# Projections of 512 tokens a matmul beside a top-256 search, with a pooling map folded into its weights

## The chip, the core and the metric

The kernel runs on one core of a Trainium2 chip. The metric is the device time of one execution in microseconds. Three runs of the kernel before took 4264.55, 4264.18 and 4262.73 us; the median is 4264.18 us.

## What is computed

One layer of an encoder over 4096 tokens of 1024 channels. Cut to what matters:

```python
h = rms_norm(x, norm_g)
q, k, v, qi, ki, wi, z_a, u_b, z_b, gates = split(h @ w_in)
# search: for each token the 256 best keys
iscore = einsum('bqhs,bqh->bqs', relu(einsum('bqhd,bsd->bqhs', qi, ki)), wi)
_, idx = top_k(where(allowed, iscore, -inf), 256)
a = softmax_attention(q, k[idx], v[idx]) * silu(z_a)
# pooling: per group g of 128 channels, window w in (2, 4, 8, 16)
pooled = (cumsum(u_b) - lagged) / count - u_b
b = (einsum('bsgc,gcd->bsgd', pooled, pool_w) * pool_scale) * silu(z_b)
y = sigmoid(g_a) * (a @ w_branch_a) + sigmoid(g_b) * (b @ w_branch_b)
out = x + y @ w_out
```

The sums over tokens and the map pool_w act on different axes, so the map may stand before or behind the sums.

## The kernel before

There are four stages. The first (up to 442.9 us of the span) norms x, projects q, k, v and the search's queries and keys, and writes h to DRAM as a high and a low part (hD). The second holds two independent pieces of work side by side: the search, and the remaining projections with their epilogues. The third is the attention, the fourth the branch products and the output. Only the second is touched, and the loads for it at the end of the first.

Products of full float32 precision are made of three: high by high, high by low and low by high.

**The projections** (`dense`). There are 28 units, each 128 columns of w_in: u and zb for four pooling groups, 16 gates a and b, and four za. They are done in sweeps over all tokens: in the first four sweeps u, zb and three gates, in the last two four gates or za. A sweep goes through the tokens in chunks of 256: two tiles h (high, low) of 1 MB are loaded for a chunk, twice buffered, and every unit of the sweep makes 24 matmuls on them, 8 k by 3 products of 128x256, into a PSUM tile pd (lines 1052 to 1054). The weights of a sweep are loaded (wraw) and split into wgh (ACT) and wgl (POOL). Those of the first sweep are loaded at the end of the first stage (`on_early`).

**Epilogues.** A gate is a sigmoid on ACT and a store (gD). The pooling (`pool`) copies u (ACT), adds shifted copies of it (POOL), subtracts the token (DVE), splits the result into ph and pl (ACT, POOL), multiplies by pool_w on PE (three matmuls of 256 columns, lines 347 to 349, with the split map wm), and multiplies by scale and silu (DVE, line 983).

**The search.** For each query block of 128 tokens, keys in pieces of 1024: PE makes the scores of a head (line 765, tile ps), ACT takes the relu (rl), DVE multiplies by the head's weight and adds into ring (line 770). POOL fills ring beforehand (iota, line 753). Blocks are collected into groups; seven rounds on ACT (line 855) and DVE find each row's threshold, and `finish` takes the last candidates (lines 883 and 884) and writes the bias, 0 or -1e30, in bf16 (line 902, on DVE), stored in pieces (biasD). A block's first threshold comes from `guess`, which needs the last block's keys, by a reload of what the first stage stored (r31, k31); its matmul is line 635.

**The order.** Every step is handed to a planner (`Plan`) with an engine, a cost, a key and the steps before it. The planner plays the program through with those costs: on each engine it starts the ready step with the smallest key whose tiles have a free buffer. What comes out is a fixed order on each engine, SP's queue of DMAs included. On the chip each engine works its order through strictly, and waits where a step is not ready. The costs and keys thus decide only the order. At the end of the stage the matmul of line 1074 counts rows whose threshold was not unique, a branch reads it, and the attention starts behind the branch.

## Time and profile before

| | |
|---|---|
| median of three runs | 4264.18 us |
| the profiled execution | 4264.02 us |
| its span | 4262.3 us |
| PE, DVE, ACT, POOL busy over the span | 97%, 75%, 55%, 45% |
| granted TensorE clock, mean | 0.987 of full speed |

The times of single instructions come from this one execution, counted from the span's start. A busy time of PE contains the drain of each matmul, which lies beside the next one: a matmul of 256 columns is shown with 0.28 us though the next starts 0.12 us after it. Distances between starts tell what PE can do. In a name such as pd<-h,wgh the tile written stands first; buffer numbers are left out. A wait is shown behind `<-` with the engine, tile and line that ended it.

### The profile page before, as it was taken

The page shows a single profiled execution, that of the slowest core. Times are in us where ns is not written, and L with a number is a line of the kernel's source. Part 1 is how long each engine was busy: PE and PEld are TensorE (multiplying, and loading weights), DVE is VectorE, ACT ScalarE, POOL GpSimd, SP SyncE. Part 2 cuts the span into 40 slices and gives each one's busy share as a digit, 9 for nine tenths or more (in the row PEclk, how much of TensorE's full clock was granted, in tenths as well). Part 3 has the DMA queues.
Part 4 walks back from the last instruction along what each step waited for, and adds up shares of the span by engine and source line. Part 5 has one row for each costly group of instructions (what it writes and reads, how often), then busy time and mean ns, then how long its engine had stood idle before and what let it go on. Part 6 is the DMA issues. An engine that isn't in the chain of part 4 may idle for free.

```text
span 4262.3 us, 76690 instructions
## 1 busy us (share of the span) xinstructions
PE 4137.7 (97%) x27746; PEld 3492.4 (82%) x27747; DVE 3217.1 (75%) x7786; ACT 2344.9 (55%) x3977; POOL 1903.4 (45%) x1717
## 2 busy tenths in 40 slices
PE   8999899999999999999799999999999999999999
PEld 7988799899999998999756666666666658999998
DVE  5554688889899888788679999999999995434342
ACT  5444588767877877887455555555555552111110
POOL 3455222323234333010047888888999991111110
PEclk9999999999999999999899999999999999999999
DMA  6666644545444446565543212212111016544442
GB/s 227 242 239 233 208 156 169 176 172 184 166 174 164 163 168 196 204 233 200 190 85 72 57 45 49 48 47 52 42 41 39 23 42 190 163 134 151 137 144 77
DMA packets 442041, 586.32 MB, mean 138 GB/s; under 512 B 148861, under 2 KB 337849, under 8 KB 437434
## 3 DMA queue, kind: packets, MB, share of 16 engines
q1 hardware_dynamic: 441658, 581.39, 42.0%
q8 instruction: 219, 3.59, 0.3%
q14 instruction: 164, 1.34, 0.1%
HBM read 388.54 MB, written 175.54 MB: 132 GB/s over the span
## 4 chain that ended last, share of the span: by engine, by line
PE 47%; DVE 1%; DMA 1%; POOL 1%; issue 0%; ACT 0%; SPq 0%; DVEq 0%; POOLq 0%; ACTq 0%
PE pv L1335 11%; PE st L1319 7%; PE ps L1280 6%; PE st L1320 6%; PE po L1533 3%; PE po L1534 3%; PE po L1535 3%; PE pa L1534 3%; PE pa L1535 3%; PE pa L1533 3%; PE st L1371 1%; PE st L341 1%; POOL acc L1350 0%; DVE tt L1323 0%; DMA maxD<-mf 0%
## 5 line engine op out<-in xcount | busy, mean ns | idle before, releaser
L1052 PE MATMUL pd<-h,wgh 128*128 128x256 f32 x3584 | 1017.7, 284 | 1.3 <-DVE zsm L972 1.3
L1053 PE MATMUL pd<-h,wgh 128*128 128x256 f32 x3584 | 1011.1, 282 | 0.0
L1054 PE MATMUL pd<-h,wgl 128*128 128x256 f32 x3584 | 1010.5, 282 | 0.0
L1350 POOL TENSOR_TENSOR acc<-acc,tt 128x1024 f32<-128x1024 f32 x388 | 928.6, 2393 | 100.4 <-ACT tt L1326 77.4
L1326 ACT ACTIVATE tt<-tt 128x512 f32<-128x512 f32 x1056 | 653.7, 632 | 554.6 <-DVE tt L1323 552.7
L1323 DVE TENSOR_TENSOR tt<-st,bT 128x512 f32<-128x512 f32 x1056 | 694.4, 686 | 74.9 <-PE st L1320 57.8
L770 DVE SCALAR_TENSOR_TENSOR ring<-rl,wi,ring 128x1024 f32<-128x1024 f32 (+7 forms) x624 | 692.1, 1153 | 12.9 <-ACT rl L768 10.3
L1052 PEld LDWEIGHTS pd<-h,wgh 128*128 128x128 f32 x3584 | 679.7, 190 | 19.7 <-issue 1.5
L1053 PEld LDWEIGHTS pd<-h,wgh 128*128 128x128 f32 x3584 | 680.4, 190 | 14.7
L1286 DVE CUSTOM_DVE_ANT_0 jk<-ps,bias 128x1024 bf16<-128x1024 f32 (+7 forms) x640 | 657.2, 1030 | 44.3 <-PE ps L1280 34.4
L1054 PEld LDWEIGHTS pd<-h,wgl 128*128 128x128 f32 x3584 | 680.3, 190 | 0.0
L768 ACT ACTIVATE rl<-ps 128x1024 f32<-128x1024 f32 (+7 forms) x624 | 539.5, 890 | 134.5 <-PE ps L765 61.9
L1335 PE MATMUL pv<-tt,vv 128*64 128x256 f32 x4224 | 525.2, 389 | 0.0
L855 ACT ACTIVATE sg<-ring,tk 128x2048 fp8e4<-128x2048 f32 (+7 forms) x322 | 486.0, 1511 | 37.8 <-DVE tk L842 21.7
L1319 PE MATMUL st<-qa,kk 128*128 128x512 f32 x1056 | 452.1, 428 | 9.7 <-DVE tt L1323 5.5
L1335 PEld LDWEIGHTS pv<-tt,vv 128*64 128x64 f32 x4224 | 279.6, 137 | 210.7 <-issue 72.4
L1320 PE MATMUL st<-qm,kl 65*128 65x512 f32 x1056 | 419.9, 398 | 3.5 <-DMA qm<-maxD 3.5
L1575 POOL TENSOR_TENSOR ga<-ga,gb 128x256 f32<-128x256 f32 x128 | 100.8, 797 | 618.7 <-DVE ga L1570 507.3
L1280 PE MATMUL ps<-kk,qa 128*128 128x512 f32 (+3 forms) x1152 | 361.9, 390 | 0.7 <-DVE mx L1286 0.7
L765 PE MATMUL ps<-kis,qT 128*128 128x512 f32 (+3 forms) x1136 | 336.3, 383 | 14.4 <-ACT rl L768 14.3
L1498 ACT ACTIVATE yh<-ga 128x256 fp32r<-128x256 f32 x128 | 53.5, 419 | 501.7 <-PE po L1534 297.5
L1319 PEld LDWEIGHTS st<-qa,kk 128*128 128x128 f32 x1056 | 199.8, 189 | 151.4 <-DVE tt L1323 47.5
(329 smaller groups left out, 7792.5 us busy)
## 6 DMA issues: line engine op xcount, KB each, us to landing
h<-hD SPq DMA_DIRECT2D x192, 1024.0 KB
hlD<-rhl SPq DMA_DIRECT2D x32, 1280.0 KB
gD<-sgm SPq DMA_DIRECT2D x256, 128.0 KB
x<-x SPq DMA_DIRECT2D x32, 512.0 KB
wraw<-w_in SPq DMA_DIRECT2D x32, 512.0 KB
hD<-hh SPq DMA_DIRECT2D x32, 512.0 KB
hD<-hl SPq DMA_DIRECT2D x32, 512.0 KB
q<-hlD SPq DMA_DIRECT2D x32, 512.0 KB
```

The source lines that it names most:

```text
L770: prev[o] = pl.add("dve", 0.1 + n * 1.04e-3, k_, lambda rl=rl, o=o, n=n, h=h: v.scalar_tensor_tensor(acc[:, o:o + n], rl.t[:, :n], self.wi ...
L1052: pe.matmul(out, wh.t[:, k], r1, start=(k == 0), stop=False)
L1053: pe.matmul(out, wh.t[:, k], r2, start=False, stop=False)
L1054: pe.matmul(out, wl.t[:, k], r1, start=False, stop=(k == KT - 1))
L1280: pe.matmul(ps.t[:, s:e], Q[b][0].t[:, 4 * g + j], kk[:, g, o + s:o + e], start=True, stop=True)
L1286: v.tensor_tensor_reduce(out=jk.t[:, :n], in0=ps.t[:, :n], in1=BI[b][0].t[:, o:o + n], scale=1.0, scalar=-3e38, op0=OP.add, op1=OP.max, ac ...
L1319: pe.matmul(s.t, kk[:, g, o], qa.t[:, hs], start=True, stop=False)
L1320: pe.matmul(s.t, kl[:, g, o], qm.t[:, hs], start=False, stop=True)
L1323: ad = pl.add("dve", 0.602, i, lambda s=s, tt=tt, r=r, kt=kt: v.tensor_tensor(tt.t[:, r], s.t, bc(bt.t[:, kt:kt + 1], [P, 4, P]), op=OP.ad ...
L1326: E[kt] = pl.add("act", 0.52, i, lambda tt=tt, r=r: act.activation(tt.t[:, r], tt.t[:, r], AF.Exp), [ad], use=[tt])
L1335: pe.matmul(pv.t[64 * f:64 * f + 64], vv[:, k, 64 * g:64 * g + 64], T[k // 2].t[:, k % 2, 2 * f:2 * f + 2], start=(k == 0), stop=(k == b))
L1350: gp.tensor_tensor(acc.t, first, tt.t, op=OP.add)
```

## The change

- A chunk has 512 tokens; the matmuls of the projections have 512 columns and their number halves. h comes in tiles of 512 KB (two k of one part, 4 KB a partition) from a ring of 13 buffers. There are 7 sweeps of four units each instead of 6; the first has gates only. The epilogues work on 512 columns.
- pool_w is no longer applied to the pooled values. For each group `through` multiplies it into w_u beforehand: 8 transposes of the raw weights, a split, 24 matmuls of 128 columns, and a second split into the unit's wgh and wgl. The wm tiles, ph, pl and the three matmuls on them are gone.
- The bias of the search is written by GpSimd instead of VectorE.
- Buffers: rl 4 to 3 (and `through` borrows two at a time), sgm 4 to 3, zsm 3 to 2 (all 512 wide), qi 2 to 1, wgh and wgl 5 to 4.
- Numbers of the planner: the key of the guess's matmul, costs, latency, the stretch STR of the search's keys.

```diff
-SGB = 4
+SGB = 3
-RL = 4
+RL = 3
+HB = 13
-STR = 0.8
+STR = 0.85
...
         if part == 0:
             self.first_w = []
-            self.first_h = self.load_h(self.early, 0, 2 * P, 1)
-        for c0 in ((C_U, C_ZB), (C_GA, C_GA + P), (C_GA + 2 * P,))[part]:
+            self.first_h = [self.load_h(self.early.tile([P, 4, 2, P], F32R, name=f"h{i}", bufs=1), i % 2, 0, i // 2)
+                            for i in range(4)]
+        for c0 in ((C_GA, C_GA + P), (C_GA + 2 * P, C_GA + 3 * P))[part]:
...
+    def load_h(self, t, part, c, kp):
+
+        self.nc.sync.dma_start(t.bitcast(F32), self.hD[part][4 * c:4 * c + 4, :, 2 * kp:2 * kp + 2].rearrange(
+            "t p k n -> p t k n"))
+        return t
...
-        s = pl.add("pe", 0.1, key, lambda: nc.tensor.matmul(pc.t[:, 0:1], ones, ks, start=True, stop=True), [s], [pc])
+        s = pl.add("pe", 0.1, 25, lambda: nc.tensor.matmul(pc.t[:, 0:1], ones, ks, start=True, stop=True), [s], [pc])
...
-                s = pl.add("dve", 0.08 + n * 0.52e-3, key, lambda bt=bt, o=o, n=n: v.tensor_scalar(
+                s = pl.add("pool", 0.1 + n * 1.2e-3, key, lambda bt=bt, o=o, n=n: po.tensor_scalar(
                     bt.t[:, :n], acc[:, o:o + n], sel.t[:, 1:2], -1e30, op0=OP.is_lt, op1=OP.mult), [s1], use=[bt, sel])
...
-        pl.run(LAT)
+        pl.run(2 * LAT)
...
-        sweeps = [[("u", g), ("zb", g)] + gates[3 * g:3 * g + 3] for g in range(4)] + [gates[12:16], gates[16:20]]
+        sweeps = [gates[0:4]] + [[("u", g), ("zb", g)] + gates[4 + 2 * g:6 + 2 * g] for g in range(4)] + [
+            gates[12:16], gates[16:20]]
...
-            ph, pq, pm = new("ph"), new("pl"), new("pd")
-            s = pl.add("dve", 0.4, k, lambda: v.scalar_tensor_tensor(
+            s = pl.add("dve", 0.65, k, lambda: v.scalar_tensor_tensor(
                 cur.t[:, 16:], cur.t[:, 16:], 1.0 / win, u.t[:, 16:], op0=OP.mult, op1=OP.subtract), [s], use=[cur, u])
-            s = pl.add("act", 0.31, k, lambda: act.activation(ph.t, cur.t[:, 16:], AF.Copy), [s], use=[cur, ph])
-            s = pl.add("pool", 0.69, k, lambda: po.tensor_tensor(pq.t, cur.t[:, 16:], ph.t.bitcast(F32), op=OP.subtract),
-                       [s], use=[cur, ph, pq])
-            s = pl.add("pe", 0.33, k, lambda: self.mm3(pm.t[:, :w2], lambda k: wm[g][0], lambda k: wm[g][1],
-                                                       lambda k: ph.t, lambda k: pq.t, 1), [s], use=[ph, pq, pm])
-            s = pl.add("dve", 0.4, k, lambda: v.scalar_tensor_tensor(
-                zs.t, pm.t[:, :w2], self.col[:, 24 + g:25 + g], zs.t, op0=OP.mult, op1=OP.mult), [s, m], use=[pm, zs])
+            s = pl.add("dve", 0.65, k, lambda: v.scalar_tensor_tensor(
+                zs.t, cur.t[:, 16:], self.col[:, 24 + g:25 + g], zs.t, op0=OP.mult, op1=OP.mult), [s, m], use=[cur, zs])
...
+        def through(g, t, raw, hi, lo, x):
+
+            pw, pwh, pwl, th, tl = new("pw"), new("pwh"), new("pwl"), new("rl"), new("rl")
...
+                s = pl.add("pe", 0.45, t, turn, [x], use=[pt, raw, th])
+                s = pl.add("act", 0.5, t, lambda pt=pt, fs=fs: act.activation(
+                    view(th)[:, fs].bitcast(F32R), pt.t, AF.Copy), [s], use=[pt, th])
+                turned.append(pl.add("dve", 0.61, t, lambda pt=pt, fs=fs: v.tensor_tensor(
+                    view(tl)[:, fs].bitcast(F32R), pt.t, view(th)[:, fs], op=OP.subtract), [s], use=[pt, th, tl]))
...
+                    for k in range(4):
+                        for y, z in ((th, pwh), (th, pwl), (tl, pwh)):
+                            pe.matmul(pt.t[:, k], view(y)[:, 4 * f + k].bitcast(F32R), z.t, start=(y is th and z is pwh),
+                                      stop=(y is tl))
+                s = pl.add("pe", 0.75, t, mm, turned + [split], use=[pt, th, tl, pwh, pwl, hi, lo])
+                s = pl.add("act", 0.5, t, lambda pt=pt, fs=fs: act.activation(hi.t[:, fs], pt.t, AF.Copy), [s],
+                           use=[pt, hi])
+                out.append(pl.add("dve", 0.61, t, lambda pt=pt, fs=fs: v.tensor_tensor(
+                    lo.t[:, fs], pt.t, hi.t[:, fs].bitcast(F32), op=OP.subtract), [s], use=[pt, hi, lo]))
+            return out
...
-                                pe.matmul(out, wh.t[:, k], r1, start=(k == 0), stop=False)
-                                pe.matmul(out, wh.t[:, k], r2, start=False, stop=False)
-                                pe.matmul(out, wl.t[:, k], r1, start=False, stop=(k == KT - 1))
-                        prev = pl.add("pe", 2.58 / DU, t, mm, lds + [have, prev], use=[pd, wh, wl] + H)
+                    def mm(kp=kp, pd=pd, wh=wh, wl=wl, H=H):
+                        out = pd.t.rearrange("p (r n) -> p r n", n=P)
+                        for k in (2 * kp, 2 * kp + 1):
+                            r1, r2 = (H[2 * kp + i].t[:, :, k % 2] for i in range(2))
+                            pe.matmul(out, wh.t[:, k], r1, start=(k == 0), stop=False)
+                            pe.matmul(out, wh.t[:, k], r2, start=False, stop=False)
+                            pe.matmul(out, wl.t[:, k], r1, start=False, stop=(k == KT - 1))
+                    prev = done[m] = pl.add("pe", 5.5 / DU, t, mm, lds[2 * kp:2 * kp + 2] + have + [prev],
+                                            use=[pd, wh, wl] + H[2 * kp:2 * kp + 2])
```

In the order of PE the start of the stage changes. Before, after the first 42 projections, L635 is the guess's matmul and L341 turns the search's first queries (qi):

```order
L1052 MATMUL pd_5331<-h_4959,wgh_4971 128x256
L1053 MATMUL pd_5331<-h_4961,wgh_4971 128x256
L1054 MATMUL pd_5331<-h_4959,wgl_4972 128x256
L635 MATMUL pd_5356<-ring 128x1
L341 MATMUL pt_5358<-identr,qi_5320 128x128 x4
L1052 MATMUL pd_5331<-h_4959,wgh_4971 128x256
```

Now, after the first 36 projections (three units on the four tiles of h loaded early), the second half of the chunk follows (its tiles h_5294 and further), with a turn of the last block's keys (k) and of the queries between:

```order
L1083 MATMUL pd_5320<-h_4963,wgl_5104 128x512
L1081 MATMUL pd_5279<-h_5294,wgh_4969 128x512
L1082 MATMUL pd_5279<-h_5306,wgh_4969 128x512
L1083 MATMUL pd_5279<-h_5294,wgl_4970 128x512
...
L341 MATMUL pt_5346<-identr,k_5264 128x128
L1081 MATMUL pd_5279<-h_5318,wgh_4969 128x512
...
L341 MATMUL pt_5357<-identr,qi_5342 128x128 x4
```

The guess's matmul (now line 632) has moved behind the first chunk and the first unit of the second.

On SP, the queue of DMAs, the same place before reads as follows (L707 and L708 reload the last block's rows and keys, L942 loads pool_w, L725 the queries):

```order
L452 DMA hlD<-rhl 128x2560
L942 DMA sgm_5270<-pool_w 128x4x128
L707 DMA r_5265<-rowD 128x296
L708 DMA k_5266<-hlD 128x128
L725 DMA qi_5320<-hlD 128x1024
L1040 DMA h_5329<-hD_82 128x2x1024
```

And now (the lines of the same steps are 702, 703 and 720, and 567 loads a tile of h):

```order
L702 DMA r_5263<-rowD 128x296
L452 DMA hlD<-rhl 128x2560
L703 DMA k_5264<-hlD 128x128
L567 DMA h_5294<-hD_82 128x4x256
L567 DMA h_5306<-hD_83 128x4x256
L567 DMA h_5318<-hD_82 128x4x256
L567 DMA h_5328<-hD_83 128x4x256
L720 DMA qi_5342<-hlD 128x1024
```

Four loads of h have moved ahead of the queries, and the load of pool_w is gone from here.

The third place is PE at a border of sweeps. Before, the pooled values of one chunk meet pool_w between projections and scores:

```order
L1054 MATMUL pd_5954<-h_5566,wgl_5106 128x256
L347 MATMUL pd_5964<-ph_5944,wm0h 128x256
L348 MATMUL pd_5964<-pl_5951,wm0h 128x256
L349 MATMUL pd_5964<-ph_5944,wm0l 128x256
L765 MATMUL ps_5968<-kis,qT_5359 128x512 x2
```

Now the preparation for the first pooling group (line 1022: rl holds the turned weights, pwh and pwl the map) stands between the last projection of the first sweep and the first of the second, L1081 with wgh_7497:

```order
L1083 MATMUL pd_7433<-h_7193,wgl_5110 128x512
L1022 MATMUL pt_7496<-pwh_5669,rl_7387 128x128
...
L760 MATMUL ps_7515<-kis,qT_7047 128x512 x2
L760 MATMUL ps_7550<-kis,qT_7047 128x512 x2
L1022 MATMUL pt_7558<-pwh_5669,rl_7387 128x128
...
L760 MATMUL ps_7600<-kis,qT_7047 128x512 x2
L760 MATMUL ps_7607<-kis,qT_7047 128x512 x2
L341 MATMUL pt_7613<-identr,qi_7076 128x128 x4
L1081 MATMUL pd_7622<-h_7229,wgh_7497 128x512
```

The 64 triples have become four such preparations, each of 8 transposes and two halves of 12 matmuls.

## Rows read from the trace of the kernel before

**Rows 1.** Busy time of each engine in the stage that the change touches: the stretch and its length, then busy us and (number of instructions) of PE, PE's weight loads, DVE, ACT and POOL, the granted clock, the busy share of the DMA engines and GB/s.

```profile
442.90:2102.60 1659.70, 1595.79 (x12325) 1535.81 (x12323) 1394.33 (x4288) 1261.02 (x1887) 403.78 (x470) 0.99 0.52 182
```

**Rows 2.** Instructions of PE and DVE in the order of time at the start and the end of the stage: start, duration, engine, line, operation; in brackets the engine's idle time before it and what ended it.

```profile
447.88 0.28 PE L1054 MATMUL pd<-h,wgl 128*128 128x256 f32 x1
466.48 0.59 PE L635 MATMUL pd<-ring 128*128 128x1 f32 x2 [18.32 <-DVE ring L608]
...
2020.99 0.41 PE L765 MATMUL ps<-kis,qT 128*128 128x512 f32 x1
...
2089.67 0.28 PE L1054 MATMUL pd<-h,wgl 128*128 128x256 f32 x1
2102.65 0.26 PE L1074 MATMUL pc<-flag,one 128*1 128x32 f32 x2 [12.70 <-DVE one L1072]
2102.00 0.48 DVE L902 TENSOR_SCALAR bt<-ring,sel 128x512 bf16<-128x512 f32 x1
```

**Rows 3.** Busy time in three stretches of the stage, columns as in rows 1; in the first PE makes nothing but projections.

```profile
2025.00:2085.00 60.00, 60.00 (x506) 60.00 (x506) 42.27 (x224) 31.46 (x69) 0.00 (x0) 1.00 0.66 233
1700.00:1900.00 200.00, 199.75 (x1561) 192.84 (x1560) 160.72 (x447) 164.67 (x239) 17.09 (x15) 1.00 0.63 216
1200.00:1400.00 200.00, 193.45 (x1478) 185.38 (x1477) 183.23 (x626) 155.44 (x228) 79.03 (x85) 0.99 0.49 172
```

**Rows 4.** The group of the projections' first product, one of three with the same count: count, busy time, mean ns of one, idle time before.

```profile
L1052 PE MATMUL pd<-h,wgh 128*128 128x256 f32 x3584 | 1017.7, 284 | 1.3 <-DVE zsm L972 1.3
```

**Rows 5.** PE in order of time: the first and the last of 18 matmuls of the output product; and a pair of score matmuls in the stage, with the projection behind it.

```profile
3904.41 0.40 PE L1533 MATMUL po<-wo,yh 128*128 128x512 f32 x1
...
3908.29 0.39 PE L1535 MATMUL po<-wo,yl 128*128 128x512 f32 x1
...
1004.25 0.64 PE L765 MATMUL ps<-kis,qT 128*128 128x512 f32 x2
1004.72 0.28 PE L1052 MATMUL pd<-h,wgh 128*128 128x256 f32 x1
```

**Rows 6.** PE in order of time: one triple of pool_w between two projections, and four transposes in the first stage.

```profile
1010.98 0.28 PE L347 MATMUL pd<-ph,wm1h 128*128 128x256 f32 x1
1011.28 0.39 PE L348 MATMUL pd<-pl,wm1h 128*128 128x256 f32 x1
...
1011.62 0.28 PE L1052 MATMUL pd<-h,wgh 128*128 128x256 f32 x1
...
400.21 0.60 PE L393 MATMUL pt<-ident,x 128*128 128x128 f32 x4
```

**Rows 7.** Groups by line over the whole span: an ACT copy of 512 columns, and groups of DVE.

```profile
L395 ACT ACTIVATE hh<-pt 128x512 fp32r<-128x512 f32 x64 | 37.4, 588 | 6.8 <-PE pt L393 6.7
L902 DVE TENSOR_SCALAR bt<-ring,sel 128x1024 bf16<-128x1024 f32 (+4 forms) x78 | 57.2, 760 | 9.5 <-DMA biasD<-bt 9.3
L976 DVE SCALAR_TENSOR_TENSOR s<-s,u 128x256 f32<-128x256 f32 x64 | 31.2, 487 | 10.8 <-POOL s L967 10.7
L983 DVE SCALAR_TENSOR_TENSOR zsm<-pd,col,zsm 128x256 f32<-128x256 f32 x64 | 30.6, 479 | 28.4 <-PE pd L349 28.1
L995 DVE TENSOR_TENSOR zsm<-pd,sgm 128x256 f32<-128x256 f32 x64 | 26.8, 422 | 21.0 <-ACT sgm L993 20.7
L972 DVE TENSOR_TENSOR zsm<-pd,sgm 128x256 f32<-128x256 f32 x64 | 26.8, 419 | 10.5 <-ACT sgm L958 10.2
L1323 DVE TENSOR_TENSOR tt<-st,bT 128x512 f32<-128x512 f32 x1056 | 694.4, 686 | 74.9 <-PE st L1320 57.8
L1524 DVE TENSOR_TENSOR o<-o,r 128x512 f32<-128x512 f32 x32 | 27.8, 870 | 3.0 <-DMA r<-invD 2.3
```

**Rows 8.** SP's issues in order of time at the start of the stage, and PE's first use of the queries.

```profile
463.45 0.33 SPq L708 DMA_DIRECT2D k<-hlD  x1
463.82 0.43 SPq L725 DMA_DIRECT2D qi<-hlD  x1
467.67 0.72 PE L341 MATMUL pt<-identr,qi 128*128 128x128 f32 x4 [0.60 <-DMA qi<-hlD]
468.19 0.54 PE L1052 MATMUL pd<-h,wgh 128*128 128x256 f32 x1
```

**Rows 9.** Groups of POOL, shapes apart, over the whole span.

```profile
L1350 POOL TENSOR_TENSOR acc<-acc,tt 128x1024 f32<-128x1024 f32 x388 | 928.6, 2393 | 100.4 <-ACT tt L1326 77.4 <-POOL acc L1350 0.5
L1353 POOL COPY acc<-tt 128x512 f32<-128x512 f32 x2 | 1.2, 611 | 37.5 <-ACT tt L1326 37.5
L979 POOL TENSOR_TENSOR pl<-s,ph 128x256 fp32r<-128x256 f32 x64 | 72.7, 1136 | 44.8 <-ACT ph L978 44.8
L959 POOL COPY u<-halo 128x16 f32<-128x16 f32 x64 | 50.6, 790 | 115.7 <-DVE s L976 99.2 <-PE pd L1054 10.1 <-PE ps L765 5.4
L967 POOL TENSOR_TENSOR s<-u 128x271 f32<-128x271 f32 x64 | 45.0, 704 | 0.0
```

**Rows 10.** PE's longest waits between 470 and 2092 us: who ended them, us in total, times, the longest.

```profile
PE ps L765 <- ACT rl L768: 14.3, 10, 4.3
```

**Rows 11.** The group of line 770 at 1024 columns, on DVE, in two stretches: 1200 to 1400 us and 1700 to 1900 us.

```profile
L770 DVE SCALAR_TENSOR_TENSOR ring<-rl,wi,ring 128x1024 f32<-128x1024 f32 x48 | 66.6, 1409 | 0.5 <-ACT rl L768 0.2
L770 DVE SCALAR_TENSOR_TENSOR ring<-rl,wi,ring 128x1024 f32<-128x1024 f32 x44 | 58.4, 1327 | 0.8 <-ACT rl L768 0.8
```

**Rows 12.** SP's longest waits over the whole span: who ended them, us in total, times, the longest.

```profile
SPq L1002 <- ACT sgm L1000: 716.0, 166, 12.0
```

More of the change, by code (lines that the diff above doesn't have):

```diff
@@ L70 @@
 IVL = 12.0
-DU = 4
 RB = 2
@@ L550, in phase1, with on_early @@
         self.es1.close()
-    def on_early(self, part, pool=None):
+    def on_early(self, part):
         nc, a = self.nc, self.a
@@ L1004, in dense, with view, turn, mm @@
+                pl.add("dma", 0.7, k, lambda: dma(self.gD[d, :, cs], sg.t), [s], use=[sg])
         W = {}
         for m, (h, l) in enumerate(self.first_w):
-            W[0, m] = (pl.have("wgh", m, h), pl.have("wgl", m, l), None)
+            W[0, m] = (pl.have("wgh", m, h), pl.have("wgl", m, l), [])
+        def through(g, t, raw, hi, lo, x):
+            pw, pwh, pwl, th, tl = new("pw"), new("pwh"), new("pwl"), new("rl"), new("rl")
+            s = pl.add("dma", 0.5, t - 20, lambda: dma(pw.t, a["pool_w"][0, g]), use=[pw])
+            s = pl.add("act", 0.2, t, lambda: act.activation(pwh.t, pw.t, AF.Copy), [s], use=[pw, pwh])
+            split = pl.add("dve", 0.2, t, lambda: v.tensor_tensor(pwl.t, pw.t, pwh.t.bitcast(F32), op=OP.subtract), [s],
+                           use=[pw, pwh, pwl])
+            def view(y):
+                return y.t.rearrange("p (k c) -> p k c", c=P)
+            turned, out = [], []
+            for f in range(2):
+                pt = new("pt")
+                fs = slice(4 * f, 4 * f + 4)
+                def turn(pt=pt, f=f):
+                    for k in range(4):
+                        pe.transpose(pt.t[:, k], raw.t[:, 4 * f + k], self.ident)
+                s = pl.add("pe", 0.45, t, turn, [x], use=[pt, raw, th])
[3 more added lines that the diff above has]
+                    view(tl)[:, fs].bitcast(F32R), pt.t, view(th)[:, fs], op=OP.subtract), [s], use=[pt, th, tl]))
+            for f in range(2):
+                pt = new("pt")
+                fs = slice(4 * f, 4 * f + 4)
+                def mm(pt=pt, f=f):
+                    for k in range(4):
+                        for y, z in ((th, pwh), (th, pwl), (tl, pwh)):
[7 more added lines that the diff above has]
+            return out
@@ L1020, in weight @@
                        [h], use=[raw, hi, lo])
-            W[s, m] = (hi, lo, l)
-        turn = 0
+            W[s, m] = (hi, lo, [l])
         t = 0.0
-        unit = 2.6
+        unit = 5.2
         prev = None
+        DU = KT // 2
         for s, mine in enumerate(sweeps):
@@ L1030, in dense @@
                     weight(s, m, kind, i, t + m * unit)
-            for c in range(S // w2):
-                H = []
-                lds = []
-                for i in range(2):
-                    if s == c == 0:
-                        H.append(pl.have(f"h{i}0", 0, self.first_h[i]))
+            for c in range(NCH):
+                H, lds = [], []
+                for n in range(KT):
+                    if s == c == 0 and n < 4:
+                        H.append(pl.have("h", n, self.first_h[n]))
+                        lds.append(None)
@@ new lines, in dense @@
+                    lds.append(pl.add("dma", 1.7, t + n // 2 * unit / DU - HLD, lambda h=h, n=n, c=c: self.load_h(
+                        h.t, n % 2, c, n // 2), use=[h]))
+                tiles = [new("pd") for _ in mine]
+                done = {}
+                order = [(m, kp) for m in range(len(mine)) for kp in range(DU)]
+                if s == c == 0:
+                    order.sort(key=lambda x: (x[0] // 3, x[1] // 2))
+                for m, kp in order:
+                    pd = tiles[m]
+                    wh, wl, have = W[s, m]
+                    def mm(kp=kp, pd=pd, wh=wh, wl=wl, H=H):
[7 more added lines that the diff above has]
+                                            use=[pd, wh, wl] + H[2 * kp:2 * kp + 2])
+                    t += unit / DU
+                    kind, i = mine[m]
+                    if kp < DU - 1 or kind == "u":
+                        continue
+                    if kind == "zb":
+                        pool(c, i, t, tiles[m - 1], pd, [done[m - 1], prev])
```

87 lines of the change are left out of this document (29 added, 58 removed).

## The prediction

> **What bounds the kernel now.** I read the stages first, then the engines inside the stage that changes, then its two ends, then single instructions.
>
> The change lies in one stage, from 442.9 to 2102.6 us: 1659.7 of the span's 4262.3 us [rows 1]. The profiled execution took 4264.02 us, 1.7 us more than its span, and the median of the runs is 4264.18; the sum below starts from 4264.0, and 0.2 us of difference is below what the runs can tell. Two activities share the stage: the projections (tiles pd, wgh, h) and the search for the 256 best keys (ps, rl, ring, tk, sg, bt). PE is busy for 1595.8 of the 1659.7 us, DVE for 1394.3, ACT for 1261.0, POOL for 403.8. So 63.9 us of PE's stage are idle, and two gaps account for 31 of them: 18.3 us at the start, and 12.7 us at the end [rows 2]. A busy PE could hide slack in its pipeline, so I take the distance between starts. In the stretch 2025 to 2085 nothing but projections runs on PE: 506 matmuls in 60.0 us are 118.6 ns each [rows 3]. The stage has 3 x 3584 = 10752 of them [rows 4]: 1275 us, three quarters of it. PE sets the stage's length, with DVE not far behind: it reaches 183 of 200 us around 1300 [rows 3].
>
> The chain of waits is no help here: cut to this stage it begins at 2108 us, behind the branch that follows the search. The end must be read from the engines' rows [rows 2]: the last score matmul starts at 2020.99, the last projection at 2089.67, the search's last DVE work at 2102.00, and PE's next instruction at 2102.65, released by DVE. The search has the last word by some 12 us.
>
> **The change, part by part.**
>
> *512 columns a matmul.* The multiplications stay the same, in half the instructions: 5376. What does one of 512 columns cost? In the last stage, 18 accumulating matmuls of this size run from 3904.41, the last starting at 3908.29: 3.88 us over 17 steps, 228 ns [rows 5]. That is the same pattern (three products per k into one bank). Against it stand the score matmuls of the stage itself: a pair takes 0.47 us, 235 ns each [rows 5]. I take 228: 5376 x 0.228 = 1226 us, 49 us less than 1275. With 235 it is 1263 us, 12 us less. The low end of the cost would be two halves without the second's fixed part; the two rows 118.6 and 228 give 9 ns of fixed part per matmul, which is the 49 us again.
>
> The Trainium skill says something else about that fixed part (TensorE: Matmul & The Clock Gate, "Wait — 56ns, not 53.3ns?"): a matmul at the full clock costs its columns over 2.4 GHz and about 2.5 ns. By that rule the halved count would give back 5376 x 2.5 ns, an estimate of 13 us, and not 49. The rows disagree with it for this kernel: 256 columns should then stand 109 ns apart, and they stand 118.6.
>
> *pool_w.* Gone are 64 triples of matmuls on ph and pl. One triple takes from 1010.98 to the next projection at 1011.62, 0.64 us instead of 0.36, since its middle member waits for POOL [rows 6]: 64 x 0.64 = 41 us. New are four preparations, each with 8 transposes and 24 matmuls of 128 columns. Four transposes take 0.60 us, the last one's drain included [rows 6]; 128 short instructions at 0.1 us are 13 us (bounds 0.06, half of a 256-column one, and 0.15, a quarter of that row: 8 to 19). They stand on PE ahead of the next sweep's first product, and the order shows that at the first two of the four sweep borders only scores lie between the preparation's halves and that product, so PE sees the chain of copy (0.59 us, rows 7), subtraction (0.69) and a turn in both engines' queues, twice. The rows have no such wait; I bound it by nothing and by two full copy-subtract-queue rounds of 3 us: 0 to 6 us a border, taken at 3, near the 2.6 us of two copies and two subtractions: 12 us. In sum 41 - 13 - 12 = 16 us less (bounds -2 to 33).
>
> *Start.* PE stops at 448.0 because the guess's matmul (L635) waits for DVE [rows 2], which waits for the reload of the last block [rows 8]. In the new order L635's counterpart stands behind the whole first chunk, but what now comes first is the second half of the first chunk, whose four loads SP issues behind the key's load (L708's counterpart). That issue is at 463.45; before, a 512 KB query tile issued at 463.82 was in use at 467.67, 3.85 us later [rows 8]. So PE resumes near 468.3, as the projections did before (468.19). It has by then done 36 matmuls of 512 (8.2 us of work) where it had done 42 of 256 (5.0): 3 us less (bounds -2 to 5). The gap stays.
>
> *End.* Behind the last score the order counts 426 matmuls of 512, 97 us, where there were 576 of 256, 68.5 us. The search needed 81 us from there to 2102; it now fits inside, and the last product ends the stage, with about 1 us to the flag's matmul. What is late next is that product. The 12.7 us gap shrinks to about 3: 9 us less (0 to 12).
>
> *Bias on POOL, epilogues.* DVE gives up L902, 57.2 us. Its four epilogue groups (115 us) become 128 instructions of 512 columns at about 0.75 us (between the 0.69 of L1323 and the 0.87 of L1524) [rows 7], 96 us, and 11 us come with the preparations: 1394 - 57 - 115 + 96 + 11 = 1329 us, 83% of the shorter stage, as before (84%). None of this is on the path while PE is the limit, so I cost it at nothing. If that cover goes, the second rival has its price. POOL gets 67,200 columns of bias (128 for each key block of the query blocks 2 to 31); one tensor read costs it 1.19 ns a column (611 ns for 512), two tensors 2.34 [rows 9]: 80 us, at most 157, in a stage where it is idle for 1256.
>
> *New waits.* PE waited 14.3 us for ACT in the scores [rows 10]. With one rl buffer less, two more lent to each preparation, and bias pieces ahead of weight splits in POOL's queue, I add 9 us (bounds -14 to 30). Tiles of h are now 13 of 512 KB, 8 to a chunk: five are loaded ahead, and the sixth waits until the chunk's last unit has let go of the first. From there PE has three quarters of that unit and two quarters of the next, 6.85 us without scores, against a load of 3.85 us. SP issues in order, and ahead of these loads stand stores that wait for ACT. I add 8 us over 55 chunk borders (bounds 0 to 137).
>
> Sum: -49 - 16 - 3 - 9 + 9 + 8 = -60 us: 4264 - 60 = **4204 us**.
>
> **The rivals.**
>
> *The stage's own 512-column rate.* If the projections run at the scores' 235 ns, 37 us of the gain stay away: 4241 us. For it: same stage, same neighbours. Against: those matmuls change bank each time, and the accumulating ones at 228 have the projections' pattern.
>
> *GpSimd brakes DVE.* POOL and DVE hold each other up: POOL's copy of 16 columns (L959) takes 790 ns on the mean and the subtraction of 256 columns (L979) 1136 ns [rows 9], where the sums of 271 columns take 704; L770 takes 1409 ns where POOL is busy for 79 of 200 us and 1327 where it is busy for 17 [rows 11]. If each bias piece holds DVE for its full length at the dear rate, DVE has 1329 + 157 = 1486 us of work; at the densest share seen (183.23 of 200) that needs 1622 us, 22 more than the forecast's 1600: 4226 us. Against it: L979, which held DVE up as well, goes. The skill's page SBUF — State Buffer, "Who interferes with whom", speaks for this rival: a DVE instruction with two inputs in SBUF and a GpSimd instruction that reads SBUF lock each other out for a whole instruction. The 790 ns agree with that.
>
> *Slower: loads late at each chunk border.* SP waits 4.3 us on the mean for a sigmoid ahead of a store (716.0 us in 166 waits, the longest 12.0) [rows 12]. Slack is 6.85 - 3.85 = 3.0 us. If the loads at each of 55 borders come 2.5 us late, the price is 137 us instead of my 8: 4333 us, slower than before. It decides from 68 / 55 = 1.2 us a border on. Against it: the stores wait only until a tile is done, and scores between the quarters lengthen the slack. Before, PE never waited for h.
>
> *Nothing changes:* the search alone carries the stage, and faster projections only wait for it. DVE's 84% and the 18.3 us of the start speak against it; the time would be about 4262.
>
> **How the numbers follow.** The forecast has 0.60, and its own range is 4170 us (no new wait, pool_w at its best bound: -49 - 33 - 3 - 9) to 4225 us (PE's waits for the search at +30). The scores' rate has 0.14, the brake 0.13, the late loads 0.09, no change 0.04. The range of 4160 to 4252 takes in the first three and leaves out the last two and the forecast's tails. A measurement here can tell 0.2%, 8.5 us, from no change. Faster: 0.60 + 0.14 + 0.13, less 0.01 for tails: 0.86. Slower: 0.09. Within 0.2%: 0.05.
>
> **What would show it.** Projections 228 ns apart in a stretch without scores (235: first rival). The last projection within 4 us of the flag's matmul, with the search done before it. PE's first gap still 17 to 20 us. Four short PE gaps at the sweep borders of the pooling, none over 6 us. No wait of the projections for h over some 10 us in all; hundreds of short ones, or a drop of the granted clock in the stage, would make the forecast wrong, as would waits of PE for ACT above 50 us. POOL's bias near 1.2 us for 1024 columns, and L770 no slower than the 1409 ns that it took around 1300; at 1500 the brake is real.

## The result, and the profile after

The changed kernel takes 4303.72 us (median of 4 runs, 4301.64 to 4308.56), beside 4264.36 us for the kernel before: ratio 1.0093, 95% interval [1.0076, 1.0111]. It is 39 us slower; 4204 us was forecast.

The first stage keeps its length, and the attention and the output keep theirs within 3 us. The second stage [rows 1] now ends with the flag's matmul (L1105) at 2137.78 us; before, at 2102.65. One row of the windows, columns as in [rows 1]:

```profile
442.90:2137.80 1694.90, 1592.80 (x6887) 1265.03 (x6886) 1357.48 (x4098) 1210.03 (x1612) 517.38 (x337) 0.97 0.61 197
```

DVE and ACT have less work than before, POOL 114 us more, and the granted clock is 0.97 where it was 0.99. What PE waits for, between 460 and 2150 us (engine, tile and line waited at, releaser: us in all, times, longest):

```profile
PE ps L760 <- ACT rl L763: 47.0, 39, 4.1
PE pd L1082 <- DMA h<-hD: 16.7, 7, 7.5
PE pd L1081 <- DMA h<-hD: 15.9, 1, 15.9
PE pt L1009 <- DVE rl L1013: 6.2, 2, 3.8
PE pt L341 <- ACT qT L731: 5.3, 3, 3.1
PE pt L1022 <- DVE rl L1013: 5.0, 1, 5.0
```

The first line answers to [rows 10]: 47.0 us, where it was 14.3. The 15.9 us are the known gap at the start. The costliest groups of POOL, by form (count, then busy us, mean ns, then idle time ahead):

```profile
L897 POOL TENSOR_SCALAR bt<-ring,sel 128x1024 bf16<-128x1024 f32 x52 | 217.6, 4184 | 310.8 <-DVE j L888 308.2
L1045 POOL TENSOR_TENSOR wgl<-wraw,wgh 128x1024 fp32r<-128x1024 f32 x20 | 49.3, 2466 | 201.4 <-ACT wgh L1044 183.7 <-PE ps L760 16.0 <-PE pt L341 1.5
L748 POOL IOTA ring<- 128x1024 int32 x50 | 48.1, 985 | 42.5 <-DVE ring L611 41.6
```

L897 is the bias. A piece of 1024 columns takes 4184 ns, all 78 pieces 279.5 us. The prediction had 80, at most 157 [rows 9]. What such a piece does is seen at 595 us, where a group's four pieces stand back to back. First POOL and SP, then PE, then DVE, each in order of time (start, us, what, idle time just before and its end):

```profile
595.42 19.02 POOL L897 TENSOR_SCALAR bt<-ring,sel 128x1024 bf16<-128x1024 f32 x4 [84.14 <-DVE j L888]
614.50 3.57 POOL L748 IOTA ring<- 128x1024 int32 x4
...
609.91 4.88 SPq L900 DMA_DIRECT2D biasD<-bt  x2
614.89 1.55 SPq L567 DMA_DIRECT2D h<-hD  x3
...
618.83 0.80 PE L1082 MATMUL pd<-h,wgh 128*128 128x512 f32 x1 [7.45 <-DMA h<-hD]
619.42 0.63 PE L1083 MATMUL pd<-h,wgl 128*128 128x512 f32 x1
619.85 0.63 PE L1081 MATMUL pd<-h,wgh 128*128 128x512 f32 x1
...
615.52 1.28 DVE L765 SCALAR_TENSOR_TENSOR ring<-rl,wi,ring 128x1024 f32<-128x1024 f32 x1 [4.47 <-POOL ring L748]
```

Two queues are held at once. POOL's index fill (L748), on which the next scores rest, stands behind the bias, and DVE waits 4.47 us for it. SP stands at the stores of the bias until 614.8; the loads of h behind it are issued at 614.89, and PE waits 7.45 us for them. After the gap the matmuls stand 0.43 us apart instead of 0.23: 512 columns in that time are 1.2 GHz, the lower of the clock's two levels. The windows around it show it, the clock in the third column from the end:

```profile
600.00:610.00 10.00, 10.00 (x44) 8.14 (x45) 10.00 (x16) 6.84 (x9) 9.82 (x3) 1.00 0.22 80
610.00:620.00 10.00, 2.55 (x9) 1.74 (x9) 4.41 (x21) 4.67 (x5) 8.00 (x5) 0.69 0.50 148
620.00:630.00 10.00, 10.00 (x37) 7.72 (x36) 2.48 (x2) 5.39 (x6) 0.00 (x0) 0.80 1.08 365
630.00:640.00 10.00, 10.00 (x45) 8.08 (x44) 7.47 (x40) 9.74 (x12) 0.00 (x0) 1.00 0.11 39
```

In the whole stage SP waits for the bias more than for any other tile but the sigmoids:

```profile
SPq L987 <- ACT sgm L985: 419.0, 103, 17.6
SPq L900 <- POOL bt L897: 244.1, 74, 15.4
```

To compare kernels below, PE's stage up to the flag's matmul is split into three, from the distances between the starts of successive matmuls: what the same matmuls take at the full clock, what is beyond that up to about double (the lower clock), and what is longer (gaps). Before: 1570.7 + 16.4 + 72.6 us. After: 1529.8 + 45.3 + 119.8. Short waits count as low clock in this split. So 41 us of work went, some 32 by the wider matmuls and 10 by pool_w (64 x 0.36 us of triples against 13 us of preparations), and 29 us of low clock and 47 of gaps came.

### The profile page after: what moved, and what is told of

Read it like the earlier page. It is cut to its first block, busy times and chain, and to the rows that moved or that the text cites. A ratio compares the mean times of both kernels' runs of the same rounds, so it can differ in the third digit from the quotient of the medians.

```text
span 4300.1 us, 64897 instructions
## 1 busy us (share of the span) xinstructions
PE 4135.8 (96%) x22306; PEld 3221.5 (75%) x22307; DVE 3180.6 (74%) x7595; ACT 2291.7 (53%) x3701; POOL 2017.7 (47%) x1584
## 5 line engine op out<-in xcount | busy, mean ns | idle before, releaser
L765 DVE SCALAR_TENSOR_TENSOR ring<-rl,wi,ring 128x1024 f32<-128x1024 f32 (+7 forms) x624 | 701.1, 1166 | 78.4 <-ACT rl L763 55.3
L1081 PE MATMUL pd<-h,wgh 128*128 128x512 f32 x1792 | 721.0, 402 | 15.9 <-DMA h<-hD 15.9
L1082 PE MATMUL pd<-h,wgh 128*128 128x512 f32 x1792 | 716.5, 400 | 16.7 <-DMA h<-hD 16.7
L1083 PE MATMUL pd<-h,wgl 128*128 128x512 f32 x1792 | 714.3, 399 | 0.4 <-DVE wgl L576 0.4
L850 ACT ACTIVATE sg<-ring,tk 128x2048 fp8e4<-128x2048 f32 (+9 forms) x322 | 485.3, 1510 | 77.6 <-DVE tk L837 36.5
L897 POOL TENSOR_SCALAR bt<-ring,sel 128x1024 bf16<-128x1024 f32 (+4 forms) x78 | 279.5, 3583 | 413.0 <-DVE j L888 407.5
L1081 PEld LDWEIGHTS pd<-h,wgh 128*128 128x128 f32 x1792 | 342.5, 191 | 94.9 <-DMA h<-hD 16.4
L1082 PEld LDWEIGHTS pd<-h,wgh 128*128 128x128 f32 x1792 | 342.0, 191 | 94.0 <-DMA h<-hD 20.7
L1083 PEld LDWEIGHTS pd<-h,wgl 128*128 128x128 f32 x1792 | 342.0, 191 | 81.8 <-DVE wgl L576 0.8
L760 PE MATMUL ps<-kis,qT 128*128 128x512 f32 (+3 forms) x1136 | 345.8, 397 | 48.1 <-ACT rl L763 47.0
```

The source lines that it names most:

```text
L765: prev[o] = pl.add("dve", 0.1 + n * 1.04e-3, k_, lambda rl=rl, o=o, n=n, h=h: v.scalar_tensor_tensor(acc[:, o:o + n], rl.t[:, :n], self.wi ...
L1081: pe.matmul(out, wh.t[:, k], r1, start=(k == 0), stop=False)
L1082: pe.matmul(out, wh.t[:, k], r2, start=False, stop=False)
L1083: pe.matmul(out, wl.t[:, k], r1, start=False, stop=(k == KT - 1))
```

## The experiments

**Who makes the bias, and where.** Four kernels tell the engine from the order.

```diff
 e1:
-s = pl.add("pool", 0.1 + n * 1.2e-3, ... po.tensor_scalar(
+s = pl.add("dve", 0.08 + n * 0.52e-3, ... v.tensor_scalar(
 e2, in the kernel before: the same line the other way round
 e9, in e1: planned as "dve", issued as po.tensor_scalar(
 e10, in the changed kernel: planned as "pool", issued as v.tensor_scalar(
```

> The changed kernel with the bias made by DVE again, as before (same instruction, same planner cost); all else as changed. Theory A (the bias takes GpSimd 4.18 us per 1024 columns where I had worked with 1.2, and what stands behind it in GpSimd's and SP's order comes late: index fills for the scores, loads of h): its stalls go, 512-column projections stay at 0.232 us. PE's gaps over 1.5 us fall from 98 us to 30 to 45, the granted clock of the stage rises from 0.97 to 0.99, time 4200 to 4235 us. Rival B (the 4 KB tiles of h with 13 buffers, and the buffers taken from the search, make the gaps): they stay whoever makes the bias, time 4285 us or more.

> The kernel before, with only the bias moved to GpSimd, at the change's planner cost. Theory A: this part alone makes it slower by 40 to 90 us, 4305 to 4355 us, with PE gaps ahead of the scores and of the projections behind each group's bias. Rival B: GpSimd has room, time 4250 to 4280 us.

> The order of e1 (planned for a bias on DVE) to the last instruction, but the bias instructions are issued to GpSimd at their places. With e1, the changed kernel and e10 this makes four: two orders, two engines. Theory A (the engine makes the loss, 4.18 us a piece): 40 to 70 us over e1, 4288 to 4318 us. Theory F (each edit only gave another order, and orders alone differ by some 50 us, as e5 and e7 did): within 15 us of e1, 4233 to 4262 us.

> The changed kernel's order to the last instruction (planned for a bias on GpSimd at 1.2 ns a column), but the bias instructions are issued to DVE. Theory A: 35 to 70 us under the changed kernel, 4234 to 4269 us. Theory F: within 15 us of the changed kernel, 4289 to 4319 us.

e1 took 4247.65 us, ratio 0.9958 [0.9941, 0.9974]; e2 4323.41, 1.0135 [1.0118, 1.0152]. With e9 and e10 each order has been run with the bias on either engine:

| order planned for | bias on DVE | bias on POOL | POOL costs |
|---|---|---|---|
| DVE | 4247.65 (e1) | 4314.15 (e9) | 66.5 |
| POOL at 1.2 ns a column | 4267.89 (e10) | 4303.72 (after) | 35.8 |

Theory A holds in both orders, at the low end of its range in e10. The order alone makes 20 us on DVE, and 10 the other way on POOL. e10 has the order of the changed kernel to the last instruction, so its waits of PE can be set beside those above:

```profile
PE ps L760 <- ACT rl L763: 43.6, 39, 4.5
PE pd L1082 <- DMA h<-hD: 3.7, 6, 0.7
```

The waits for h fall by 13 us, and DVE's waits for index fills (L748), 19.0 us in the changed kernel, are gone; the waits for ACT hardly fall. e10's stage is 29 us shorter (2109.1 against 2137.8 us); what is left of that is low clock and other gaps.

In e2 theory A has the time right and the place wrong: not the scores wait longer (5.8 us for ACT), but pool_w's second product (L348) for its split on POOL, 40.0 us where it was 12.1. It is POOL's own queue again, with another step behind the bias.

The parts of e1's stage are 1530.4 + 26.5 + 84.9 us; so with the bias back the change gains 18 us in the stage, far less than the 60 forecast, and e1 missed its own range by 13 us. What PE waits for in e1:

```profile
PE ps L760 <- ACT rl L763: 37.6, 43, 3.1
PE pd L1081 <- DMA h<-hD: 15.8, 1, 15.8
PE pt L1009 <- DVE rl L1013: 4.4, 1, 4.4
PE pd L1082 <- DMA h<-hD: 3.5, 4, 1.1
```

The waits for h inside the stage go from 16.7 to 3.5 us: they were the stores' of the bias, as e10 shows in one order. The waits for ACT stay above twice the 14.3 of [rows 10].

**A true cost in the plan, and the store in another queue.**

```diff
 e3: -pl.add("pool", 0.1 + n * 1.2e-3, ...
     +pl.add("pool", 0.1 + n * 3.5e-3, ...
 e4: -pl.add("dma", 1.0, key, ... dma(self.biasD ...
     +pl.add("pool", 0.1, key, ... po.dma_start(self.biasD ...
```

> The changed kernel, bias on GpSimd, but the planner is told 0.1 us + 3.5 ns a column for it in place of 1.2 ns (measured: 4.18 us for 1024 columns), so that the order is planned with it. If the loss comes from an order built on a wrong cost, most of it comes back: 4225 to 4265 us. If a slow instruction in GpSimd's one queue delays the others wherever it stands, or rival B holds: 4285 us or more.

> The changed kernel, bias on GpSimd, but its store is issued by GpSimd right behind the bias, and no longer by SP. If SP standing at the store, with the loads of h behind it, makes the stalls, the projections' waits for h (33 us) and the gaps ahead of them go: 4235 to 4275 us. If the index fills and weight splits behind the bias on GpSimd itself make them, gaps ahead of the scores (L760) stay: 4280 us or more. Rival B: no change, 4300 us.

e3: 4277.81 us, 1.0027 [1.0018, 1.0037], 26 us better than the changed kernel and between the two expectations. That an order which knows the price hides part of it fits, but isn't shown: the order is new, and e1 and e10 lie 20 us apart by order alone. e4: 4317.24 us, 1.0123 [1.0107, 1.014], as its second expectation says. With the store off SP, PE's waits for h inside the stage do go, from 16.7 to 1.2 us, so SP's stand at the store made them; but the waits for ACT in the scores grow from 47.0 to 69.3 us, and the time doesn't fall. POOL's own queue stays behind the bias, and the order is new too; how much SP's wait counts by itself isn't settled by it.

**The bias's form by itself**, with the search over:

```diff
+po.tensor_scalar(mb[0], mi, one, -1e30, op0=OP.is_lt, op1=OP.mult)   # the bias's form
+po.tensor_scalar(mf[0], mi, one, -1e30, op0=OP.is_lt, op1=OP.mult)   # into f32
+po.tensor_scalar(mf[1], mi, -0.5, 1.5, op0=OP.mult, op1=OP.add)
+po.tensor_scalar(mb[1], mi, -0.5, 1.5, op0=OP.mult, op1=OP.add)
+po.tensor_scalar(mf[2], mi, one, None, op0=OP.is_lt)
+po.tensor_copy(mb[2], mi)
```

> e1 with eight instructions on GpSimd and one on DVE added behind the search, on 128x1024 (one on 128x512), to measure the bias's form by itself; the added results are not used. The bias's form took 3.70 to 5.47 us in the changed kernel. If the form itself is dear: 3.7 us alone too, with DVE idle; the copies 1.2 us. If the comparison is dear: multiply-add with constants takes 1.2 to 2.5 us, and the compare alone 3.7. If the bf16 output is dear: the same comparison into f32 takes 1.2 to 2.5 us. If two scalar operations are dear: one operation takes half. If it was only DVE's traffic: about 1.2 us alone.

```profile
2089.24 4.20 POOL L1109 TENSOR_SCALAR mb<-mi,one 128x1024 bf16<-128x1024 f32 x1 [149.65 <-DVE tot L1122]
2093.53 3.70 POOL L1110 TENSOR_SCALAR mf<-mi,one 128x1024 f32<-128x1024 f32 x1
2097.30 1.05 POOL L1111 TENSOR_SCALAR mf<-mi 128x1024 f32<-128x1024 f32 x1
2098.32 1.05 POOL L1112 TENSOR_SCALAR mb<-mi 128x1024 bf16<-128x1024 f32 x1
2099.35 2.85 POOL L1113 TENSOR_SCALAR mf<-mi,one 128x1024 f32<-128x1024 f32 x1
2102.15 1.04 POOL L1114 CAST mb<-mi 128x1024 bf16<-128x1024 f32 x1
```

The form is dear by itself, 3.70 us; the first piece, 4.20, ran beside a DVE instruction. The bf16 output costs nothing, and two operations as such need not: multiply and add by constants takes 1.05 us in either type. What costs is the comparison with a scalar of each partition (2.85 us alone); the multiplication behind it adds 0.85. Which of the two, the comparison or the scalar from a tile, wasn't tried.

**What else took the gain: buffers, pace, step size.** All from e1 but e6 and e12, which are the kernel before.

```diff
 e5:  -RL = 3, HB = 13        +RL = 4, HB = 12
 e6:  -RL = 4                 +RL = 3
 e7:  -STR = 0.85             +STR = 0.8
 e11: -STR = 0.85             +STR = 0.9
 e12: -STR = 0.8              +STR = 0.85
 e13: -for k in (2 * kp, 2 * kp + 1): 6 matmuls a step
      +one k, 3 matmuls a step
```

> Bias on DVE as in e1, and the fourth rl buffer of the search given back, paid for with one tile of h (12 instead of 13, the same memory). Theory C (with the bias on DVE, what still keeps the gain small is the search: ACT cannot evict scores since DVE still holds one of three rl buffers, and PE's 37.6 us of waits for ACT come from that): PE's waits for ACT fall to 10 to 25 us, ACT's idle time ahead of L763 behind DVE's ring add falls from 106 us to below 50, time 4222 to 4238 us. Rival D (that is the order's pace, not the buffers): waits stay above 30 us, 4243 to 4252 us. Rival E (the thirteenth tile of h is needed): waits of the projections for h rise above 20 us, 4250 us or more.

> The kernel before with three rl buffers in place of four, nothing else. Theory C: PE's waits for ACT rise from 14.3 us by 10 to 25 us and the kernel by as much: 4272 to 4292 us. Rival D: within 6 us of before, 4258 to 4270 us.

> Bias on DVE as in e1, and the search paced as before in the order (STR 0.8 in place of 0.85), buffers as changed. Rival D: PE's waits for ACT fall below 25 us, 4225 to 4240 us. Theory C: within 8 us of e1, 4240 to 4256 us.

> e1 (bias on DVE) with the search paced slower in the order (0.9 for 0.85; e7 had 0.8 and came to 4301 us). In e1 the search's last score stands 93 us ahead of the last projection. If the pace as such counts (a search pushed too early fills ACT and DVE, and PE waits for them): PE's waits for ACT fall to 10 to 30 us and the time to 4215 to 4240 us. If the orders only scatter: anywhere from 4240 to 4310 us, with waits for ACT of 37 to 70 us.

> The kernel before with the change's pace of the search (0.85 for 0.8) and nothing else: how far an order alone moves the old kernel. If orders scatter by 50 us there too: 4220 to 4310 us but not within 10 us of 4264. If the old kernel, with finer steps of PE (0.7 us in place of 1.4 us), takes a new order well: 4250 to 4280 us.

> e1 with PE's projections planned in steps of three 512-column matmuls (0.7 us, as before) in place of six (1.4 us). Theory G: PE's waits for ACT fall from 37.6 us to 10 to 20, away from the borders too, 4215 to 4235 us. Theory H: the borders still cost 30 us or more, 4240 to 4310 us, as orders scatter.

| | us | ratio to before, 95% | full-clock work + low clock + gaps | PE's waits for ACT |
|---|---|---|---|---|
| e5 | 4308.54 | 1.0103 [1.0086, 1.012] | 1527.9 + 45.7 + 128.6 | 71.6 |
| e7 | 4301.20 | 1.0089 [1.0072, 1.0106] | 1529.1 + 38.3 + 126.1 | 69.4 |
| e11 | 4314.04 | 1.0106 [1.0089, 1.0122] | 1528.5 + 38.5 + 145.0 | 65.3 |
| e13 | 4336.50 | 1.0168 [1.0151, 1.0185] | 1529.0 + 42.3 + 165.2 | 83.3 |
| e6 | 4293.05 | 1.0069 [1.0052, 1.0086] | 1569.9 + 16.1 + 98.6 | 19.3 |
| e12 | 4270.37 | 1.0007 [0.9998, 1.0017] | 1570.3 + 20.7 + 71.6 | 10.4 |

e12 came as its second expectation says; of the others most fell beside both. A fourth rl buffer doesn't mend e1 (C falls), and it wasn't h either that made e5 slow: its waits inside the stage are 14 us (E falls). e6 is slower by its end, where the flag waits 36.3 us for a late search, and hardly by waits for ACT. Neither pace helps (D falls), nor finer steps (G falls). Yet PE's work is the same in e5, e7, e11 and e13, and the old kernel hardly minds its new pace. The new structure loses 54 to 89 us to e1 by its order (in e5 with other buffers). Some of it lies where pool_w is multiplied into w_u. For each kernel four windows hold the 60 us around its own first four borders of sweeps, from 40 us ahead of the new sweep's first product to 20 us behind it. They begin at 719, 1010, 1301 and 1608 us in the kernel before, where pool_w is not multiplied into w_u, at 665, 906, 1144 and 1380 in e1, and at 679, 934, 1168 and 1427 in e11. Their sums, busy time of PE first, in this order:

```profile
sum 240.00, PE 221.02 PEld 211.18 DVE 212.44 ACT 166.44 POOL 106.82; mean PE 55.25 PEld 52.79 DVE 53.11 ACT 41.61 POOL 26.71
```

```profile
sum 240.00, PE 216.36 PEld 171.55 DVE 192.00 ACT 164.95 POOL 69.63; mean PE 54.09 PEld 42.89 DVE 48.00 ACT 41.24 POOL 17.41
```

```profile
sum 240.00, PE 189.77 PEld 142.65 DVE 176.88 ACT 128.32 POOL 52.55; mean PE 47.44 PEld 35.66 DVE 44.22 ACT 32.08 POOL 13.14
```

PE stands 19 us in them before, 24 in e1, 50 in e11, and the clock falls there: e1 has 0.83 in its second window, e11 0.72. So the borders of e1 cost little more than those of the old kernel. Those of e11 cost 27 us more than e1's, of the 66 by which e11 is slower; the rest lies in the clock and elsewhere. The order shows a reason for the borders. There are four weight slots, and the plan gives the splits of other weights the highest priority, so w_u gets the last slot that the old sweep frees. In e11 the first border's second set of transposes, its two sets of products and the next sweep's projections then have nothing but scores and one turn of queries between them, and each rests on a copy and a subtraction. PE's waits there, from 695 to 721 us, are 7.3 us in the scores for ACT and 0.5 each for two subtractions; ACT in turn waits for DVE's adds, which hold the rl buffers.

**The preparation, left out or moved.**

```diff
 e16: -if kind == "u": ... through(...); return
 e19: -W[s, m] = (hi, lo, through(i, t - 12, ...
      +W[s, m] = (hi, lo, through(i, t - 24, ...
      -h = pl.add("act", 0.95, t - WSP, ... AF.Copy), [x], ...
      +h = pl.add("act", 0.95, t - WSP, ... AF.Copy), [x] + made[:1], ...   # made[0]: w_u's first products
 e17, in e1: "wgh": (5, ...), "wgl": (5, ...), HB = 11, through(i, t - 30, ...
 e21: e19 with STR = 0.8      e22: e19 with STR = 0.9
```

> e1 (bias on DVE) without multiplying pool_w into w_u: w_u is split like the other weights, and pool_w is left out of the output. Theory H (the preparation of w_u at the four borders stops PE: its hi and lo get the last weight slot that the old sweep frees, so only scores stand between its halves and the sweep's first product, while it holds two of the three rl buffers): the loss within 40 us of the borders falls from 37 us to below 8, PE's own work by about 20 us, time 4180 to 4212 us. Theory G (PE's coarser steps, or the buffers, make the waits): only its own work goes, 4222 to 4240 us.

> e1 with the preparation kept, but planned 24 us ahead of the border in place of 12, and the splits of the sweep's other weights planned behind it, so that w_u takes the first weight slot that comes free. In the order, projections of the old sweep then stand between its halves. Theory H: loss at the borders falls from 37 us to 5 to 20, time 4215 to 4240 us. Theory G: 4240 us or more, with waits for ACT as in e1 or longer.

> e1 with a fifth pair of weight buffers as in the kernel before, paid for by two tiles of h (11 in place of 13), and the preparation planned 30 us ahead of the border. Theory H: loss at the borders 5 to 20 us, 4210 to 4240 us. Rival E (tiles of h are short): waits of the projections for h rise from 19 to 40 us or more, 4250 us or more.

> e7 (bias on DVE, pace 0.8, 4301 us) with the preparation of w_u mended as in e19. Theory H (the late preparation is what makes these orders slow): most of the 72 us between e7 and e19 goes, 4225 to 4260 us. Theory I (the pace shifts the search as a whole, and the preparation is a side matter of some 20 us): 4275 to 4300 us, PE's waits for ACT still above 55 us.

> e11 (bias on DVE, pace 0.9, 4314 us) with the preparation of w_u mended as in e19; in this order projections stand between its halves at three of the four borders, at the first only scores. Theory H: 4225 to 4270 us, with 15 us or more of loss left only at the first border. Theory I: 4285 to 4315 us, PE's waits for ACT above 55 us.

e16: 4219.92 us, 0.9892 [0.9876, 0.9909], 28 under e1 and between the two theories. The two profiled executions lie 24 us apart: 13 us of PE's own work, 10 of low clock and gaps in the stage. In its own windows (655, 880, 1108 and 1355) PE stands 21 us without any preparation, of 24 in e1; with the low clock, by the distances between matmuls, the loss there is some 35 us, of 44. So H's "below 8" was wrong: in e1's order the preparation's stalls are only some 10 us.

e19: 4228.91 us, 0.992 [0.9904, 0.9937], the fastest kernel here that leaves nothing out: 1529.4 + 23.1 + 72.1 us. e22: 4245.96, 0.9952 [0.9936, 0.9969], 68 us under e11, by the same edit. The windows at their own borders (659, 885, 1117 and 1358 in e19; 663, 889, 1118 and 1347 in e22) show it:

```profile
sum 240.00, PE 226.50 PEld 181.53 DVE 202.79 ACT 161.92 POOL 71.24; mean PE 56.62 PEld 45.38 DVE 50.70 ACT 40.48 POOL 17.81
```

```profile
sum 240.00, PE 221.23 PEld 177.03 DVE 209.37 ACT 162.86 POOL 61.36; mean PE 55.31 PEld 44.26 DVE 52.34 ACT 40.72 POOL 15.34
```

PE stands 13 us at e19's borders and 19 at e22's, of 24 in e1 and 50 in e11. e19 does better there than e16 does without a preparation, and has less low clock and gaps in the whole stage (95 us against 102). So its gain can't be the preparation's stall alone; the rest comes with the new order.

e21: 4278.77 us, 1.0033 [1.0021, 1.0044], 22 under e7 and 50 over e19, nearer to theory I. PE stands 39 us in its windows (656, 902, 1161 and 1399), where e7 has 46 (682, 922, 1179 and 1422). The edit mended the first border, 1.4 us from 14.0, and none of the others: from 1155 to 1205 PE waits 9.7 us for ACT, and 4.9 and 2.9 us inside the preparation, though projections stand between its halves in the order. So H is borne out at paces 0.85 and 0.9, by the time and by the windows; why 0.8 stays slow is open, and since orders scatter as they do, two cases of three don't prove it. e17 (4376.57 us, 1.0257 [1.024, 1.0274]) went by rival E. With 11 tiles PE waits for h 45 times, 44.1 us:

```profile
PE ps L760 <- ACT rl L763: 83.8, 83, 6.2
PE pd L1082 <- DMA h<-hD: 44.1, 45, 4.3
PE pd L1081 <- DMA h<-hD: 19.5, 5, 15.9
```

## Why the prediction was wrong

**Bias on POOL: the step that failed.** It priced 67,200 columns at 1.19 ns from a copy, at most 2.34 from a two-tensor sum, and then cost them at nothing, as POOL was idle for 1256 us. The rows of the operation itself say 4.2 ns (279.5 us / 67,200), outside both bounds: neither row compares with a scalar of each partition. And "idle" was the wrong cover. POOL has room in the sum, but it works in order, and index fills stand behind the bias; SP, which stores it, has the loads of h behind that. Price 36 us (order of the change) to 66 us (order of e1). This turned the sign, but it is not all of the miss: e10, the same order with the bias on DVE, still takes 4267.89 us, 64 above the forecast.

The Trainium skill (GPSIMD Engine Reference, "Engine selection") calls GpSimd's one-input elementwise work roughly line-rate. The copy and the multiply-add agree with that (1.04 and 1.05 us for 1024 columns); the bias's form, also with one tensor, doesn't (3.70 us), and here the measurement decides.

**512 columns: mechanism right, size off by 17 us.** In a stretch without scores the projections stand 0.232 us apart (median from 2040 to 2130 us), not 0.228:

```profile
2059.64 0.40 PE L1083 MATMUL pd<-h,wgl 128*128 128x512 f32 x1
2059.87 0.40 PE L1081 MATMUL pd<-h,wgh 128*128 128x512 f32 x1
2060.11 0.40 PE L1082 MATMUL pd<-h,wgh 128*128 128x512 f32 x1
2060.34 0.40 PE L1083 MATMUL pd<-h,wgl 128*128 128x512 f32 x1
```

The whole stage's median is 0.232 us too, beside 0.119 for 256: 5376 x 0.232 against 10752 x 0.119 is 32 us, not 49. The rate lies between the forecast's 0.228 and the first rival's 0.235. The po matmuls [rows 5] were too fast a model, the scores beside them the nearer one.

The Trainium skill's 2.5 ns of fixed part (TensorE: Matmul & The Clock Gate, "Wait — 56ns, not 53.3ns?") would have given an estimated 13 us; the 32 measured disagree with it as [rows 5] did.

**pool_w: work right, wait too steady.** The 64 triples that went had taken 43 us by the distances between matmuls (41 forecast), and the preparations' PE work is 13 us, as predicted (1530.4 with, 1517.2 without). The 12 us of waits at four borders came to about 10 in e1, but not in every order: in e11 PE stands 50 us at the borders, 19 after the edit of e22, and the stage has 183.5 us of low clock and gaps against 112.8. The rows of the order had shown that only scores lie between the halves at two borders; the prediction priced the chain and not what the stall takes with it: the clock, and the search, which has lent two of three rl buffers.

**Waits for ACT, late h, start, end.** Waits for ACT went from 14.3 to 47.0 us (37.6 with the bias on DVE), where 9 more were predicted, at most 30. h: 8 us predicted, 16.7 measured, 3.5 once the bias was off POOL; the slower rival had the right queue (a store ahead of the loads on SP), but the wrong store and 7 places, not 55. Start: PE's gap is 15.9 us, from 18.3, near the 3 us less of the sum, though under the 17 to 20 us named as a sign. End: the last projection stands 1.9 us ahead of the flag's matmul, with the last score at 2035.3, as predicted.

**The clock was not in the sum.** It went from 16.4 to 45.3 us of low clock: 29 us that follow gaps. The prediction had named a drop of the granted clock, and waits for h over some 10 us, as signs that it would be wrong; both came.

**The other rivals.** GpSimd's brake hardly shows in L765: 1329 ns for 1024 columns in the stretch 1200:1400, under the limit of 1409, and 1166 on the mean where it took 1153. It does show in L890, a DVE instruction of one column that runs beside the beginning of the bias: 858 ns on the mean of 30, where e10 has 160. Those 21 us of DVE are small beside the rival's 157 and part of the bias's price. "Nothing changes" is out.

From 4204 to 4304 us, then: 36 for the bias; 20 for the changed kernel's order against e1's (PE stands 32 us at e10's borders, windows from 674, 914, 1150 and 1392, and 24 at e1's; the rest of the 20 isn't placed); 17 for the 512-column rate; 14 for waits for ACT, and 10 for low clock, as they are left in e1. That is 97 of 100 us. The 36 and the 20 are shown by swaps; the other three are read from e1's trace and may overlap, so their sum is an estimate. With the bias on DVE and the preparation moved, the same change gives 35 us.

## What to carry to other kernels

Before work is moved to an idle engine, find that very form in a trace, with its operands, or measure it; then ask what stands behind it in that engine's order and in the queue that stores its result. A step prepared at a border belongs where other matmuls still cover its chain of copies, and buffers must come free early enough for that; here this helped at two paces of three. And try a structure with two or three orders before judging it: here 66 us lay between e1 and e11, two orders with the same work on each engine.
